# One RWKV-7 layer's key stage: a chain without GpSimd products, decays a tile ahead, and the triangles of the later heads by ranges of chunks

## The chip, the cores and the metric

The kernel runs on one core of a Trainium2 chip. The metric is the device time of one execution in microseconds (us); lower is better. The core has a matrix engine (TensorE, PE in the rows; PEld is its weight load), three elementwise engines (VectorE or DVE, ScalarE or ACT, GpSimd or POOL) and a sync engine (SyncE or SP) that does nothing but issue DMAs. Each engine has a queue of its own that it works off in order; DMAs can also be issued by ACT and POOL, and then stand in their queues.

## The reference

A decoder step of two layers over a prompt of 1024 tokens and 8 sampled tokens; the change lies in the first layer, RWKV-7 time mixing, with 32 heads of 64 channels. Cut to what matters here:

```python
r, k, v, z = einsum('pbtd,pde->pbte', mixed, w_in)          # four projections, 1024 -> 2048
w_log = -softplus(-(w0 + tanh(xw @ w1) @ w2)) - 0.5
decay = exp(-exp(w_log)); a = sigmoid(a0 + (xa @ a1) @ a2)
kk = k * k_k; kk = kk / max(norm(kk), 1e-12)                # per head
k = k * (1 + (a - 1) * k_a)
def step(S, (r, w, k, v, a, b)):                            # a = -kk, b = kk * a
    sa = S @ a
    S = S * w + outer(sa, b) + outer(v, k)
    return S, S @ r
S_fin, y = scan(step, S0, ...)                              # 1024 steps, per head
bonus = sum(rh * kh * r_k) * vh
```

The kernel does the scan in 32 chunks of 32 tokens. Inside a chunk the step is solved with the inverse of a unit triangular 32x32 matrix per head and chunk ("the triangles"), 32 x 32 of them.

## The kernel before

The layer runs in stages: r, v, then k with everything that the recurrence needs (the stage of the change), then the recurrence over 32 chunks, with the projection z spread between its steps as filling for PE. All projections are fp32 products made of three fp32r matmuls (high and low halves).

**The loop of k.** Channels are split into 16 tiles `ct` of 128 (two heads each). One pass of the loop (`for ct in range(KI - 1)`) does three tiles' work at once: `kproj(ct + 1)` (24 steps of three matmuls, spread by `steps`) and `ua(ct + 1)` (the two small projections `u` for decay and a) on PE for the next tile; the elementwise chain of tile ct; `score` (products of the rows, tile `sc`), `rows` (transposes, `tr`) and `bonus` (`bo`) of tile ct - 1. The chain of a tile: `norm` (sums of squares `ss`, maximum on VectorE, logarithm and exponential on ScalarE, each with a table load), `newkey`, `decay2` (running products of the decays over a chunk), `raw_rows`, `unit`, `unit2`, `unit_rows`; they write the rows `RA` and `BK`, which exist once. `unit` also issues the product r*k of `bonus` on GpSimd (line 821); `bonus` of the tile reads it one pass later. The program order is written by hand, and no scheduler moves anything.

**The triangles.** Tile pairs (4 heads x 32 chunks = 128 partitions) are inverted together by `inverse`: 31 steps of one multiplication (L1081) and one addition (L1083) on blocks of up to 256 elements per partition. Seven pairs run on GpSimd, a step at three of four places in `steps`, the eighth on VectorE after the loop (the tail). A pair is loaded from `n_d` and stored to `u_d` or `u2_d`.

**Into the recurrence.** `phase_r` loads, for each chunk, `xs_d` and `ra_d` (tile `xz`), `u_d`/`u2_d` (tile `U`) and `v_d` (into tile `st`). 24 of the steps of z (`ZK`) are done in the tail and 27 (`ZPRE - ZK`) ahead of the first chunk. `sample_step`, the 8 sampled tokens' state update on GpSimd and VectorE, advances by one step at each of six places of a chunk.

## Time and profile before

| | |
|---|---|
| time, median of 3 runs | 2971.76 us (2968.67 to 2973.62) |
| the profiled execution: its own time | 2943.64 us |
| its span, first to last instruction | 2941.9 us |
| busy: PE / PEld / DVE / ACT / POOL | 2696.3 / 2418.5 / 1672.7 / 1361.2 / 1430.5 us |
| the loop of k, tile 0's logarithm to tile 15's | 463.7 us |
| PE, DVE, POOL busy in it | 380.4, 402.6, 368.6 us |

The profiled execution is 28.1 us (0.9%) below the median of the timed runs. The busy time of PE is modelled from pipelined records, so it overstates how close PE is to its peak. Tiles are named by number: "tile 5" is the pass of the loop with ct = 5.

### The profile page before, as it was taken

How to read it: one execution, taken by the hardware profiler on the slowest of the kernel's cores; microseconds unless marked ns; L12 is line 12 of the kernel's file. 1: busy time of each engine (PE TensorE's matmuls, PEld its weight loads, DVE VectorE, ACT ScalarE, POOL GpSimd, SP SyncE). 2: the span in 40 equal slices, each digit the busy share in tenths (PEclk: the TensorE clock that was granted, in tenths of full speed). 3: DMA queues.
4: the chain of work that ended last, by engine and by line, in shares of the span. 5: the costliest groups of instructions: out<-in, count | busy, mean ns of one | idle time of the engine just before them, and what ended most of it. 6: DMA issues, size and time to landing. Idle time of an engine off the chain costs nothing.

```text
span 2941.9 us, 64866 instructions
## 1 busy us (share of the span) xinstructions
PE 2696.3 (92%) x26386; PEld 2418.5 (82%) x26386; DVE 1672.7 (57%) x2952; ACT 1361.2 (46%) x2886; POOL 1430.5 (49%) x1385
## 2 busy tenths in 40 slices
PE   7999998878786788888879999999999999899998
PEld 7999997766675677767769989999999999666897
DVE  7232117989797756666574144127777777533414
ACT  7232226767675444445454335225555555333423
POOL 3322121699999566663245455313444433475342
PEclk9999999989898899999989999999999999999999
DMA  4332334667677899999777552322111111586525
GB/s 157 120 126 76 96 88 113 162 145 174 155 162 190 206 223 218 227 227 210 175 228 225 173 123 78 107 83 83 54 56 54 56 52 55 157 274 201 179 90 187
DMA packets 567501, 423.80 MB, mean 144 GB/s; under 512 B 176260, under 2 KB 515649, under 8 KB 567074
## 3 DMA queue, kind: packets, MB, share of 16 engines
q1 hardware_dynamic: 473954, 336.06, 42.5%
q10 hardware_dynamic: 79648, 38.42, 4.9%
q0 software_dynamic: 13600, 45.16, 4.9%
q8 instruction: 208, 3.41, 0.5%
q14 instruction: 91, 0.75, 0.1%
HBM read 281.69 MB, written 133.35 MB: 141 GB/s over the span
## 4 chain that ended last, share of the span: by engine, by line
PE 57%; POOL 7%; DVE 7%; DMA 5%; issue 4%; ACT 3%; SPq 1%; ACTq 0%; DVEq 0%; POOLq 0%
PE p L62 8%; PE zb L62 6%; PE sc L62 6%; PE bo L62 5%; PE wop L62 4%; PE o L62 4%; POOL Xt L1081 2%; POOL X L1083 2%; PE s L62 2%; PE q L62 2%; PE pt L2156 2%; PE v L62 2%; PE k L62 1%; PE pt L2575 1%; PE bt L62 1%
## 5 line engine op out<-in xcount | busy, mean ns | idle before, releaser
L76 POOL TENSOR_TENSOR wl<-wr,wh 128x1024 fp32r<-128x1024 f32 x32 | 84.3, 2654 | 288.0 <-ACT wh L71 269.5
L1081 POOL TENSOR_TENSOR Xt<-N,X 128x31 f32<-128x31 f32 (+15 forms) x217 | 187.0, 862 | 27.2 <-DMA N<-n_d 11.0
L1083 POOL TENSOR_TENSOR X<-X,Xt 128x31 f32<-128x31 f32 (+15 forms) x217 | 183.8, 847 | 17.0
L71 ACT CAST pth<-pt 128x256 fp32r<-128x256 f32 (+1 forms) x320 | 108.2, 355 | 128.8 <-DVE ptl L76 74.8
L1289 DVE TENSOR_TENSOR st<-s,gC 64x512 f32<-64x512 f32 x128 | 88.2, 689 | 131.6 <-PE s L62 129.2
L62 PE MATMUL p<-mh,w3h 128*128 128x344 f32 x384 | 149.6, 390 | 6.2 <-issue 5.0
L76 DVE TENSOR_TENSOR ptl<-pt,pth 128x256 fp32r<-128x256 f32 (+1 forms) x320 | 120.9, 391 | 27.0 <-ACT pth L71 25.0
L62 PE MATMUL p<-ml,w3h 128*128 128x344 f32 x384 | 130.8, 341 | 5.1 <-issue 2.9
L62 PE MATMUL p<-mh,w1h 128*128 128x344 f32 x360 | 134.9, 375 | 0.0
L62 PE MATMUL p<-mh,w3l 128*128 128x344 f32 x384 | 127.1, 337 | 3.7 <-issue 3.7
L62 PE MATMUL r<-mh,wh 128*128 128x344 f32 x384 | 124.7, 325 | 4.6 <-ACT tf L483 4.6
L62 PE MATMUL r<-mh,wl 128*128 128x344 f32 x384 | 124.1, 323 | 0.0
L62 PE MATMUL r<-ml,wh 128*128 128x344 f32 x384 | 123.9, 323 | 0.0
L2139 ACT ACTIVATE pr<-sc,mx 128x128 f32<-128x128 f32 (+7 forms) x128 | 95.4, 745 | 53.1 <-DVE mx L2136 51.6
L62 PE MATMUL p<-mh,w1l 128*128 128x344 f32 x360 | 119.9, 333 | 0.0
L62 PE MATMUL p<-ml,w1h 128*128 128x344 f32 x360 | 119.8, 333 | 0.0
L2136 DVE TENSOR_REDUCE mx<-sc 128x1 f32<-128x128 f32 (+7 forms) x128 | 96.7, 755 | 3.2
L1305 ACT COPY y<-y 32x256 f32<-32x256 f32 x256 | 93.2, 364 | 10.7 <-PE y L62 7.1
L1276 ACT COPY st<-sa 32x256 f32<-32x256 f32 x128 | 46.4, 362 | 111.1 <-PE sa L62 100.7
L1950 DVE TENSOR_TENSOR zbr<-zb,RS 128x384 f32<-128x384 f32 (+1 forms) x48 | 24.6, 515 | 126.1 <-PE zb L62 123.8
L62 PEld LDWEIGHTS s<-st,xz 128*64 128x64 f32 x2048 | 72.6, 148 | 27.9 <-issue 20.9
L2041 POOL TENSOR_TENSOR qp<-qp,rope 128x256 f32<-128x256 f32 (+1 forms) x30 | 22.4, 747 | 145.8 <-DMA qsw<-qp 122.4
(1237 smaller groups left out, 9944.9 us busy)
## 6 DMA issues: line engine op xcount, KB each, us to landing
xs_d<-XS SPq DMA_DIRECT2D x64, 512.0 KB, 5.9
xz<-xs_d SPq DMA_DIRECT2D x64, 512.0 KB, 9.0
wr<-in_a_w_in_dram SPq DMA_DIRECT2D x17, 1024.0 KB, 6.1
ra_d<-RA SPq DMA_DIRECT2D x32, 512.0 KB, 7.3
...
```

Of the source, the lines that this page charges most:

```text
L62: PE.matmul(out, lhsT=lhsT, rhs=rhs, start=start, stop=stop)
L71: ACT.copy(out, in_)
L76: (eng or V).tensor_tensor(out, in_, hi_.bitcast(F32), ALU.subtract)
L1081: eng.tensor_tensor(t3, N_[:, s_:s_ + 1, s_ + 1:].to_broadcast([P, a, b]), X_[:, r0:r1, s_:s_ + 1].to_broadcast([P, a, b]), ALU.mult)
L1083: eng.tensor_tensor(X_[:, r0:r1, s_ + 1:], X_[:, r0:r1, s_ + 1:], t3, ALU.add)
L1276: (V.tensor_copy if j % 2 else ACT.copy)(d, pa[j % 2][ts(j, 32)])
L1289: V.tensor_tensor(ST[s_][1 - c % 2][rows, qs, :], p3[rows], gC[rows, qs, c:c + 1].to_broadcast([64, 8, 64]), ALU.mult)
L1305: ACT.copy(ys[B][ts(ci, 32), a:a + 2].rearrange("p a s d -> p (a s d)"), p_[ts(j, 32), 0:256])
L2136: V.tensor_reduce(mx, sc[:, :W], AX.X, ALU.max, negate=True)
L2139: ACT.activation(pr[:, :W], sc[:, :W], AF.Exp, bias=mx, accum_out=sm)
L2156: PE.transpose(pt[:, ts(q, P)], pr[:, ts(g + q, P)], ident)
L2575: PE.transpose(p_[:, ts(r, P)], pg[:, r, ts(c, P)], ident)
```

## The change

Eight things are changed. (1) The product r*k goes from GpSimd to VectorE, to the end of the pass (`rk`). (2) GpSimd cuts the low halves of k's weights (`w1l`) instead of VectorE. (3) The decays: a running sum (`CS`) on VectorE and two exponentials on ScalarE replace two exponentials and two running products; they, and the first half of `newkey`, are made for tile ct + 1 at the end of pass ct. (4) The small projections' low weights are laid out over 128 rows instead of 64. (5) `rows` leaves PSUM by one copy per group instead of four, into a tile `TR` of its own, and `xs_d` becomes two arrays with 64 elements for each channel row and chunk. (6) `score` and `rows` stand group by group in the pass. (7) The triangles of tiles 0 to 7 are made in the loop, four tiles at a time (`GROUPS`), with two triangles behind each other in every instruction; those of tiles 8 to 15 are sorted by ranges of 8 chunks, two ranges on VectorE in the tail and two on GpSimd beside the recurrence (`side`), ahead of `sample_step`. (8) The chunk's load reads `xs_d` by four DMAs instead of two.

```diff
-    xs_d = scr("xs_d", (2, NC, 64, P * KI))
+    xs_d = [scr(f"xs{i}_d", (2, KI, 64, NC, 64)) for i in range(2)]
...
-    u_d = scr("u_d", (NC, 4, C, 6, C))
-    u2_d = scr("u2_d", (NC, 2, 4, C, C))
+    u_d = scr("u_d", (NC, 4, C, 4, C))
+    u2_d = [scr(f"u2_{i}_d", (8, 4, C, 4, C)) for i in range(4)]
...
-                lo(b_, raw[:, 4 * hf:4 * hf + 4], a)
+                lo(b_, raw[:, 4 * hf:4 * hf + 4], a, G if i == 1 else V)
...
+            def lcut2(ct):
+                lo(st[ct]["l2"], st[ct]["l2r"], st[ct]["s2"])
...
-                        mm(p_[:, :NQ], d["s2"][i], th2[i][:, nsl[n]], True, False)
-                        mm(p_[:, :NQ], d["l2"][me], th2[i][me, nsl[n]], False, True)
+                        mm(p_[:, :NQ], d["s2"][:, i], th2[i][:, nsl[n]], True, False)
+                        mm(p_[:, :NQ], d["l2"][:, i], th2[i][:, nsl[n]], False, True)
...
-                ACT.activation(Wp[:, :, 1:33], c3(TW), AF.Exp, bias=cneg, scale=-0.5 * CDEC)
-                ACT.activation(Wi[:, :, 1:33], c3(TW), AF.Exp, bias=cpos, scale=0.5 * CDEC)
+                ACT.activation(CS[:, :, 1:33], c3(TW), AF.Identity, bias=ones[:, 0:1])
...
-                V.tensor_tensor_scan(fl(Wp), fl(Wp), fl(E0), 0.0, ALU.mult, ALU.add)
-                V.tensor_tensor_scan(fl(Wi), fl(Wi), fl(E0), 0.0, ALU.mult, ALU.add)
-                V.tensor_copy(gC[:, ct, :], Wp[:, :, 32])
...
+                V.tensor_tensor_scan(fl(CS), fl(E0), fl(CS), 0.0, ALU.mult, ALU.add)
+                ACT.activation(fl(Wp), fl(CS), AF.Exp, scale=-0.5 * CDEC)
+                ACT.activation(Wi, CS[:, :, 1:33], AF.Exp, scale=0.5 * CDEC)
+                ACT.activation(gC[:, ct, :], CS[:, :, 32], AF.Exp, scale=-0.5 * CDEC)
...
+                GG = st[ct]["GG"] = kp.tile([P, T], F32, tag="GG", name=f"GG{ct}")
+                ACT.activation(GG, st[ct]["TA"], AF.Identity, bias=dv[:, 3, ct:ct + 1], scale=dv[:, 2, ct:ct + 1])
...
-                V.tensor_scalar(GG, TA, dv[:, 2, ct:ct + 1], dv[:, 3, ct:ct + 1], ALU.mult, ALU.add)
-                V.tensor_scalar(TA, TA, -0.5, -0.5, ALU.mult, ALU.add)
-                V.tensor_tensor(GG, GG, d["K"], ALU.mult)
+                V.tensor_tensor(d["GG"], d["GG"], d["K"], ALU.mult)
...
-                G.tensor_tensor(d["K"][:, :S], d["R"][:, :S], d["GG"][:, :S], ALU.mult)
+            def rk(ct):
+                d = st[ct]
+                V.tensor_tensor(d["K"][:, :S], d["R"][:, :S], d["GG"][:, :S], ALU.mult)
...
-                V.tensor_tensor(d["TA"], d["TA"], d["RN"], ALU.mult)
+                V.scalar_tensor_tensor(d["TA"], d["TA"], 1.0, d["RN"], ALU.add, ALU.mult)
...
-                        SY.dma_start(n_d[ct, s_, HC[hf]].rearrange("c s t -> s c t"), d["nts", hf][r0:r0 + 32])
+                        nt = d["nts", hf][r0:r0 + 32]
+                        if ct < 8:
+                            SY.dma_start(n_d[ct, s_, HC[hf]].rearrange("c s t -> s c t"), nt)
+                            continue
+                        for i in range(2):
+                            SY.dma_start(n2_d[2 * hf + i, ct - 8, s_].rearrange("c s t -> s c t"), nt[:, ts(i, 8)])
...
-                for u in range(2):
...
-                    ACT.copy(x4[64:128, :, u, :], v4[src, :, 0, :])
-                    ACT.copy(x4[0:64, :, u, :], v4[src, :, 1, :])
...
+                ACT.copy(d["TR", hf][:, :, ts(g % 2, 4)], p_.rearrange("p (m s d) -> p s m d", m=4, s=2))
...
-                        SY.dma_start(xs_d[s_, HC[hf]][:, :, ts(ct, P)].rearrange("c r t -> r c t"),
-                                     d["XS", hf][64 * s_:64 * s_ + 64])
+                        SY.dma_start(xs_d[1][s_, ct][:, HC[hf]], d["XS", hf][64 * s_:64 * s_ + 64])
+                        for u in range(2):
+                            SY.dma_start(xs_d[0][1 - s_, ct][:, c0 + 8 * u:c0 + 8 * u + 8], d["TR", hf][ts(u, 64), s_])
...
-                    if u % 4 != 3:
-                        next(pend[0], None)
+                    due[0] += rate[0]
+                    while due[0] >= 1:
+                        due[0] -= 1
+                        istep()
...
+            GROUPS = {4: [(0, 0), (0, 1)], 8: [(0, 2), (0, 3)]}
+
+            def whole(qs, eng=G):
+                for _ in range(3):
...
+                while late:
+                    late.pop(0)()
+                rate[0] = 0.36
...
+                yield from inverse(qs, (*bufs, ivp.tile([P, C * C // 2], F32, tag="Xt", name=f"Xt{q}")), eng, late)
...
+                nm = norm(ct)
                 if p >= 0:
                     score(p, 0)
+                    rows(p, 0)
+                    bonus(p)
+                steps(kpr, 2)
+                run(take(nm, 2))
+                steps(kpr, 1)
+                run(nm)
+                newkey2(ct)
...
                     score(p, 1)
...
+                    rows(p, 1)
+                steps(kpr, 2)
...
                 raw_rows(ct, 0)
...
                 unit(ct)
...
-                if ct % 2 == 0 and p >= 0:
-                    run(pend[0])
-                    fresh = whole(p // 2)
-                    next(fresh)
...
                 unit2(ct)
                 unit_rows(ct, 0)
                 ra_store(ct, 0)
+                steps(kpr, 2)
+                if p >= 0:
+                    score(p, 2)
+                    rows(p, 2)
+                steps(kpr, 3)
+                if p >= 0:
+                    score(p, 3)
+                    rows(p, 3)
+                if ct in GROUPS:
+                    iq.append(whole(GROUPS[ct]))
+                if late and not iq:
+                    late.pop(0)()
...
                 raw_rows(ct, 1)
                 unit_rows(ct, 1)
                 ra_store(ct, 1)
+                rk(ct)
                 sample(ct)
                 rload(ct + 1)
+                for u in range(6):
+                    steps(kpr, 1)
+                    next(up)
+                run(up)
+                if ct + 2 < KI:
+                    lcut(ct + 2)
+                decay(ct + 1)
+                steps(kpr, 2)
+                newkey(ct + 1)
+                if ct + 2 < KI:
+                    lcut2(ct + 2)
+                decay2(ct + 1)
...
+                steps(kpr, 6)
...
+            iv7 = whole([(1, 0), (1, 1)], V)
+            for _ in range(4):
+                next(iv7)
...
             run(iv7)
-            late[1]()
...
+            late.pop(0)()
...
+    def inverse(qs, bufs, eng, late):
...
+        n = len(qs)
+        N_, X_ = (t_.rearrange("p n (a b) -> p n a b", b=C) for t_ in bufs[:2])
+        xf, tm = bufs[1:]
+        for i, (by_chunk, q) in enumerate(qs):
+            src = n2_d[q] if by_chunk else n_d[2 * q:2 * q + 2]
+            SY.dma_start(bufs[0][:, i], src.rearrange("k s c a b -> (k s c) (a b)"))
+        eng.memset(xf, 0.0)
+        eng.memset(xf[:, :, 0:1024:33], 1.0)
         yield
...
-                    eng.tensor_tensor(t3, N_[:, s_:s_ + 1, s_ + 1:].to_broadcast([P, a, b]),
-                                      X_[:, r0:r1, s_:s_ + 1].to_broadcast([P, a, b]), ALU.mult)
-                    eng.tensor_tensor(X_[:, r0:r1, s_ + 1:], X_[:, r0:r1, s_ + 1:], t3, ALU.add)
...
+            a, b = s_ + 1, C - 1 - s_
+            t4 = tm[:, :n * a * b].rearrange("p (n a b) -> p n a b", n=n, b=b)
+            eng.tensor_tensor(t4, N_[:, :, s_:s_ + 1, s_ + 1:].to_broadcast([P, n, a, b]),
+                              X_[:, :, 0:a, s_:s_ + 1].to_broadcast([P, n, a, b]), ALU.mult)
+            eng.tensor_tensor(X_[:, :, 0:a, s_ + 1:], X_[:, :, 0:a, s_ + 1:], t4, ALU.add)
...
-            for j in range(4):
...
-                    G.dma_start(u2_d[:, q - 6, j], X_[ts(j, 32)])
+            for i, (by_chunk, q) in enumerate(qs):
+                for j in range(4):
+                    if by_chunk:
+                        for x in range(4):
+                            rows = slice(8 * (4 * x + j), 8 * (4 * x + j) + 8)
+                            {0: (SY, ACT), 1: (G, G)}.get(q, (SY, SY))[j % 2].dma_start(u2_d[q][:, j, :, x], X_[rows, i])
+                    else:
+                        SY.dma_start(u_d[:, j, :, q], X_[ts(j, 32), i])
...
-                    SY.dma_start(X[rows, :, 128 - 128 * s_:256 - 128 * s_], xs_d[s_, c].rearrange("r (a t) -> r a t", t=P))
+                    o = 128 - 128 * s_
+                    for i, x in enumerate((c // 16 * 16 + c % 2 * 8 + c % 16 // 2, c)):
+                        SY.dma_start(X[rows, :, o + 64 * i:o + 64 * i + 64], xs_d[i][s_, :, :, x].rearrange("a r t -> r a t"))
...
-                    SY.dma_start(U[:, 0:6], u_d[c].rearrange("j a q t -> (j a) q t"))
+                    SY.dma_start(U[:, 0:4], u_d[c].rearrange("j a q t -> (j a) q t"))
...
-                    SY.dma_start(Us[c][:, 6:8], u2_d[c].rearrange("q j a t -> (j a) q t"))
+                    SY.dma_start(Us[c][:, 4:8], u2_d[c // 8][c % 8].rearrange("j a q t -> (j a) q t"))
...
-            sp = rx.enter_context(tc.tile_pool(name="spl", bufs=1, side="right", reuse_waits="tile"))
-            sg = sample_step(sp, lambda n: psum("tr", n, 1), osT, SM)
...
+            def side():
+
+                with ExitStack() as vx:
+                    vp = vx.enter_context(tc.tile_pool(name="ivr", bufs=1, side="right", reuse_waits="tile"))
+                    for r in (2, 3):
...
+                        out = []
+                        yield from inverse([(1, r)], bufs, G, out)
+                        yield
+                        yield
+                        out[0]()
+                sp = rx.enter_context(tc.tile_pool(name="spl", bufs=1, side="right", reuse_waits="tile"))
+                yield from sample_step(sp, lambda n: psum("tr", n, 1), osT, SM)
...
-                    next(sg, None)
+                    run(take(sg, 2 if c > 11 and i % 2 else 1))
```

On GpSimd, in the loop of k, before (a pair's triangles, and the product of tile 9; `N`, `X`, `Xt` are a triangle, its inverse and a scratch tile):

```order
L1081 TENSOR_TENSOR Xt3_7014<-N3_7012,X3_7013 128x255
L1083 TENSOR_TENSOR X3_7013<-X3_7013,Xt3_7014 128x17x15
L821 TENSOR_TENSOR K9_6804<-R9_7047,GG9_7193 128x1024
L1081 TENSOR_TENSOR Xt3_7014<-N3_7012,X3_7013 128x252
L1083 TENSOR_TENSOR X3_7013<-X3_7013,Xt3_7014 128x18x14
```

and now, around tile 11's weights:

```order
L1107 TENSOR_TENSOR Xt0203_6907<-N0203_6905,X0203_6906 128x270
L1109 TENSOR_TENSOR X0203_6906<-X0203_6906,Xt0203_6907 128x2x5x27
L76 TENSOR_TENSOR w1l11_0_7156<-w1r11_6961,w1h11_0_7136 128x512
L1107 TENSOR_TENSOR Xt0203_6907<-N0203_6905,X0203_6906 128x312
L1109 TENSOR_TENSOR X0203_6906<-X0203_6906,Xt0203_6907 128x2x6x26
L1107 TENSOR_TENSOR Xt0203_6907<-N0203_6905,X0203_6906 128x350
```

The product is gone from the queue, the low weights stand in it, and the blocks are two triangles wide (128x270 is 2 x 135).

On VectorE, the end of a pass, before (tile 3; `XS` is the next pass):

```order
L838 COPY SM_117<-GG3_5169 128x8
L76 TENSOR_TENSOR w1l5_1_5408<-w1r5_5182,w1h5_1_5406 128x512
L73 CAST l2h0_5_5440<-l2r5_5112 64x128
L76 TENSOR_TENSOR l2l5_5442<-l2r5_5112,l2h0_5_5440 64x128
L73 CAST l2h1_5_5441<-l2r5_5112 64x128
L76 TENSOR_TENSOR l2l5_5442<-l2r5_5112,l2h1_5_5441 64x128
L855 TENSOR_TENSOR XS3_0_5457<-sc3_0_5459,ctab_75 128x8x64
```

and now:

```order
L825 TENSOR_TENSOR K3_4778<-R3_4977,GG3_5041 128x1024
L842 COPY SM_122<-R3_4977 128x8
L842 COPY SM_122<-RN3_5120 128x8
L842 COPY SM_122<-GG3_5041 128x8
L843 TENSOR_SCALAR SM_122<-TA3_4985 128x8
L76 TENSOR_TENSOR l2l5_5324<-l2r5_5074,l2h5_5323 128x256
L798 SCALAR_TENSOR_TENSOR CS_4228<-E0_4229,CS_4228 128x1056
L860 TENSOR_TENSOR XS3_0_5373<-sc3_0_5375,ctab_80 128x512
```

The weights' cuts have left, the product r*k has come, and the running sum of tile 4 stands ahead of the next pass; `CS` waits for ScalarE, which reads the small projections.

On ScalarE, after the loop, where the eighth triangle's step ends, before:

```order
L872 COPY XS15_1_9451<-tr15_3_9573 64x4x64
L873 COPY XS15_1_9451<-tr15_3_9573 64x4x64
L1041 COPY bT_9654<-bo_4260 32x256 x4
L767 COPY zrow0_9680<-p3_0_0_9384 128x344
L767 COPY zrow0_9680<-p3_0_1_9388 128x344
L767 COPY zrow0_9680<-p3_0_2_9392 128x344
```

and now (`u2_0` takes the inverses of chunks 0 to 7, `X1011`):

```order
L880 COPY TR15_1_9132<-tr15_2_9127 128x2x256
L880 COPY TR15_1_9132<-tr15_3_9134 128x2x256
L1118 DMA u2_0_d_70<-X1011_9056 8x32x32 x8
L1068 COPY bT_9244<-bo_4264 32x256 x4
L769 COPY zrow0_9270<-p3_0_0_8941 128x344
L769 COPY zrow0_9270<-p3_0_1_8945 128x344
L769 COPY zrow0_9270<-p3_0_2_8949 128x344
```

Eight stores that wait for the last triangle now stand ahead of the copies of `bo` on ScalarE; eight more stand on SyncE and sixteen on GpSimd.

## Rows read from the trace of the kernel before

**Rows 1.** Busy time by stretch: tile 1, tile 5, the loop, the recurrence

```profile
core 0: us, PE busy (x) PEld busy (x) DVE busy (x) ACT busy (x) POOL busy (x), PEclk, DMA share, GB/s
490.70:515.80 25.10, 24.57 (x244) 20.08 (x242) 23.52 (x37) 21.39 (x44) 2.75 (x1) 1.00 0.73 169
601.70:630.80 29.10, 26.18 (x242) 21.53 (x242) 27.12 (x36) 21.63 (x43) 27.00 (x30) 0.94 0.75 166
467.40:931.10 463.70, 380.44 (x3536) 309.00 (x3535) 402.63 (x523) 315.33 (x625) 368.59 (x403) 0.91 0.65 156
...
1060.00:1480.00 420.00, 369.09 (x8153) 306.21 (x8151) 270.86 (x464) 204.09 (x520) 219.48 (x146) 0.94 0.91 210
```

**Rows 2.** Waits of PE in the loop: total, times, longest

```profile
PE bo L62 <- POOL K L821: 53.3, 9, 13.7
PE ss L62 <- DVE RN L783: 23.0, 10, 5.0
```

**Rows 3.** Timeline of VectorE and GpSimd in tile 1: start, duration

```profile
502.82 2.75 POOL L821 TENSOR_TENSOR K<-R,GG 128x1024 f32<-128x1024 f32 x1 [20.57 <-DVE RN L819]
...
503.26 3.41 DVE L825 TENSOR_TENSOR TA<-TA,RN 128x1032 f32<-128x1032 f32 x1
```

**Rows 4.** Timeline of PE in tile 13, around a pair of small products

```profile
876.20 0.32 PE L62 MATMUL u<-th,l2h 128*128 128x344 f32 x1
876.45 0.42 PE L62 MATMUL u<-th,l2l 64*128 64x344 f32 x1
876.80 0.42 PE L62 MATMUL p<-mh,w1h 128*128 128x344 f32 x1
```

**Rows 5.** Groups of ScalarE in tile 1: busy us, mean ns

```profile
L873 ACT COPY XS<-tr 64x256 f32<-64x256 f32 x8 | 2.9, 368 | 0.1
...
L71 ACT CAST w1h<-w1r 128x512 fp32r<-128x512 f32 x2 | 1.2, 618 | 0.0
L790 ACT ACTIVATE Wp<-TW,cneg 128x1024 f32<-128x1024 f32 x1 | 1.1, 1149 | 0.0
...
L785 ACT ACTIVATE RN<-RN 128x1032 f32<-128x1032 f32 x1 | 1.1, 1071 | 0.0
```

**Rows 6.** Groups of VectorE in tile 1

```profile
L798 DVE TENSOR_TENSOR_SCAN Wi<-Wi,E 128x1056 f32<-128x1056 f32 x1 | 2.3, 2332 | 0.0
...
L819 DVE SCALAR_TENSOR_TENSOR RN<-K,vecA,RN 128x1032 f32<-128x1032 f32 x1 | 1.3, 1284 | 0.0
```

**Rows 7.** The triangles on GpSimd, from the page's groups

```profile
L1081 POOL TENSOR_TENSOR Xt<-N,X 128x31 f32<-128x31 f32 (+15 forms) x217 | 187.0, 862 | 27.2 <-DMA N<-n_d 11.0
L1083 POOL TENSOR_TENSOR X<-X,Xt 128x31 f32<-128x31 f32 (+15 forms) x217 | 183.8, 847 | 17.0
```

**Rows 8.** The product r*k in the loop, a group of GpSimd

```profile
L821 POOL TENSOR_TENSOR K<-R,GG 128x1024 f32<-128x1024 f32 x15 | 37.3, 2484 | 67.5 <-DVE RN L819 67.5
```

**Rows 9.** Timeline of VectorE in the tail

```profile
971.73 0.67 DVE L1081 TENSOR_TENSOR Xt<-N,X 128x31 f32<-128x31 f32 x1
...
991.42 0.42 DVE L1081 TENSOR_TENSOR Xt<-N,X 128x256 f32<-128x256 f32 x1
```

**Rows 10.** Timeline of PE and GpSimd in the tail

```profile
972.44 1.16 PE L1045 MATMUL boT<-ctab,bT 32*128 32x32 f32 x8
...
986.79 0.32 PE L62 MATMUL p<-mh,w3h 128*128 128x344 f32 x1
...
1003.84 1.94 POOL L1091 DMA_DIRECT2D u_d<-X  x4 [8.62 <-DVE X L1083]
```

**Rows 11.** State products on VectorE: 1000 to 1050, then all (first to last start)

```profile
L1289 DVE TENSOR_TENSOR st<-s,gC x10: 682/689/695, 1007.6 to 1047.8; 64x512 f32<-64x512 f32 x10
...
L1289 DVE TENSOR_TENSOR st<-s,gC x128: 682/690/696, 1007.6 to 1486.8; 64x512 f32<-64x512 f32 x128
```

**Rows 12.** DMA queues, 1200 to 1300: packets, MB, time as share of 16 engines

```profile
q1 hardware_dynamic: 26511, 17.29, 75.7%
q10 hardware_dynamic: 13947, 4.88, 21.1%
```

156 lines of the change are left out of this document (57 added, 99 removed).

## The prediction

> **What bounds the kernel now.** I read the busy times by stretch first, then the waits of PE in the loop of k, then the timeline around the waits, since the change lies in that loop, the tail behind it and the recurrence. The loop takes 463.7 us for 15 periods, 30.9 each, with PE busy for 380.4 and GpSimd for 368.6 [rows 1]. In tile 1, where GpSimd has only the product r*k, a period lasts 25.1 and PE is busy for 24.6; in tile 5, where it also makes triangles, 29.1, with GpSimd busy for 27.0 [rows 1]. So there are two limits: PE where GpSimd is quiet, and GpSimd where it is not. The waits name the link: PE stood for 53.3 us in nine waits at `bonus` until the product on GpSimd was done, and for 23.0 in ten at the sums of squares until VectorE had read the ones before [rows 2]. The product is short (2.48 on the mean [rows 8]) but stands behind the steps of a triangle, and everything behind `bonus` in PE's queue stands behind it.
>
> GpSimd also slows VectorE. In tile 1 the product ran from 502.82 to 505.57, and a multiplication that VectorE began at 503.26 ended at 506.67, 1.1 after the product [rows 3]; its like takes 1.28 [rows 6], so it stood for some 2.1. The Trainium skill ("SBUF — State Buffer", section "SBUF: two separate sides") says that GpSimd and VectorE instructions with two inputs in SBUF take turns at a shared port for whole instructions; these two rows agree.
>
> **The change part by part.**
>
> *The product on VectorE.* It costs VectorE about 1.28 (same width as in [rows 6]) and takes away the 2.1 of standing. The 53.3 of waiting at `bonus` go, unless VectorE is late in turn: the product now ends pass ct, and `bonus` reads it at the start of pass ct + 1, behind `score` and `rows`.
>
> *PE per tile.* A small product starts its high half at 876.20, its low half at 876.45 and hands over at 876.80: 0.60 for two matmuls, and the one behind lasts 0.42 [rows 4]. In the tail 81 matmuls of the same width take 986.79 - 973.6 (972.44 + 1.16), 0.16 each [rows 10]. If the 64-row weights make the difference, 128 rows save 0.60 - 0.32 on the pair and 0.1 behind it, 0.38 times 6 = 2.3 per tile; the bounds are nothing and 2.3, and I take all, since the gap stands only at that shape. Four blocks of `score` and `rows` instead of two cost two more changes of shape each way, 0.5 by the same rows. PE would need 24.6 - 2.3 + 0.5 = 22.8.
>
> *ScalarE per tile.* It is busy for 21.4 [rows 1]. Sixteen copies at 0.37 (5.9), two exponentials of 1.15 and two small casts (0.6) go; four copies of 512 columns come (0.62 each at most, as the cast of that width), a copy into `CS` and two exponentials (1.15 each), `newkey` (1.07), a small exponential and a cast (0.7) [rows 5]. 21.4 - 8.8 + 7.7 = 20.3.
>
> *The ring from tile to tile.* ScalarE's queue is now closed through VectorE in two places. After the exponential of `norm`, VectorE makes `unit` and `unit2` (1.28 each), two rows and the next mask (0.65 each, half the width), 4.5 in all [rows 6], before ScalarE can copy `score`'s third group; it has 1 us of copies meanwhile, so it stands for 3.5. The running sum takes 2.33 [rows 6] between `CS` and the exponentials of the decays, with 1.3 of other ScalarE work beside it, so it stands for 1. The square of the next K is queued behind that. A period is then 20.3 + 4.5 = 24.8, say 24.9, above PE's 22.8. VectorE's own sum falls below it: 23.5 [rows 1] less one running product (2.33), the standing (2.1), the weights' cuts and the two scalings that ScalarE or a fused instruction takes over (some 3), plus the product: 17 to 18. So I expect PE to wait for ScalarE's and VectorE's chain for 2 us in a quiet tile; the bounds of a quiet period are 22.8 (all of that hidden) and 26.
>
> *Triangles in the loop.* They now fill tiles 4 to 11. Now 62 instructions take 0.855 each on the mean of 176 elements [rows 7]; the product is the row for 1024, 2.48 [rows 8]. On the line between, 352 elements cost 1.19, so four tiles' triangles cost 74 against 106 for two pairs. At 0.36 steps of 24 per tile they spread over four tiles: 18.4 each, plus two cuts of 512 at 1.35, 21.1. That fits a period. In the middle, where a block has 512 elements, 8.6 steps cost 24 and the cuts 2.7: just over it, so the weights may come late by a few us once per group. VectorE pays for GpSimd's company: 27.1 against 23.5 [rows 1], a sixth, on the 7 us of it that lie in the ring. 24.9 + 1.2, and 1 for late weights: 27.0 with the bounds 25 and 30. GpSimd no longer delays `bonus`; what is queued behind a late weights' cut is PE's next tile, and that is the last link between them.
>
> The loop: 7 x 24.9 + 8 x 27.0 = 390, **-73** (with the bounds' ends -104 to -42).
>
> *Ahead of the loop* the running sum and the exponentials of tile 0 stand uncovered in part: **+2**.
>
> *Tail, VectorE.* Two running products (4.7) and two scalings leave the stretch ahead of the last triangle, the product comes: -5. The triangle itself took from 971.73 to 1003.5 [rows 9, 10]. 256 elements cost 0.42 late in it [rows 9]; most of that scales with the elements, so twice the blocks at, by estimate, 0.55 for each of 62 with their gaps are 34: +2. Together **-3** (-10 to +4).
>
> *Tail, behind the triangle.* Before, its stores waited on GpSimd (8.62 us [rows 10]) and nothing was queued behind them but a fill. Now eight wait on ScalarE and eight on SyncE. Behind them on ScalarE stand the copies of `bo`, the evacuation of z and the fills for the first chunk; behind `bo`'s transposes on PE stand 27 steps of z, which before ran from 973.6 to 986.79 beside the triangle [rows 10]. On SyncE the loads of chunks 0 and 1 stand behind them. So what took 4.0 us (1003.5 to the first state product at 1007.6 [rows 10, 11]) now takes 5 for the stores' issues (by estimate: four took 1.94 [rows 10], and the second four wait for the first to land), 1.5 for the copies, 1.2 for the transposes, 13.2 for the 27 steps and 4.0 as before, 25 in all: **+21** (+5, should PE have other work, to +28).
>
> *First chunks.* Two chunks took 40.2, against 479.2 / 31.5 = 15.2 for one on the mean [rows 11]; the loads now have those 20 us of PE's work as cover: **-8** (0 to -10).
>
> *Recurrence.* Two triangles of 62 instructions (53 us each at 0.855) on GpSimd, whose busy share is half [rows 1]; the step of the samples follows in the later chunks. The state products on VectorE took 682 to 696 ns whatever stood on GpSimd [rows 11], so I cost it at nothing (0 to +10). The loads: the same bytes in pieces of 256 B instead of 512 B. Queue 10, which carries `ra_d` in 256 B pieces, moved 4.88 MB in 21.1% of 16 x 100 us, 14.5 bytes per ns; queue 1, with the 512 B pieces, 17.29 MB in 75.7%, 14.3 [rows 12]. Time goes by bytes, so: nothing. The Trainium skill ("DMA: Bandwidth & Descriptors", section "Specifications") wants at least 512 B per transfer for line rate; these two rows do not show that loss, and by the rule alone the sum would end on the other side, as in the third rival.
>
> Sum: -73 + 2 - 3 + 21 - 8 = -61. Against the profiled execution's 2943.6 us that is 2883; it lies 28.1 below the median of the runs, and I carry the difference over: 2971.8 - 61 = **2911 us**.
>
> **The rivals.**
>
> *The ring is shorter than I add up* (copies overlap, ScalarE is never behind): quiet periods at PE's 22.8, busy ones at 25: 7 x 22.8 + 8 x 25 = 360, -104 in the loop, -92 in all: 2880. For it: ScalarE has 20.3 of work in such a period. Against it: its queue is in order and has two waits for VectorE.
>
> *GpSimd stays the bound of busy tiles*: double blocks cost double (1.71), 106 per group and 11 of cuts with waits, 117 in four tiles, 29.3, as tile 5 is now. 8 x 29.3 + 7 x 24.9 = 409, -55, and -43 in all: 2929. For it: the mean of 0.855 holds the turns with VectorE, and those grow with an instruction's length. Against it: VectorE has a quarter less to do.
>
> *Slower: the small pieces cost as much as large ones.* At 14.3 bytes per ns and engine a chunk's 1 MB takes 4.6 us of 16 engines; in half pieces at the price of whole ones 9.2. The engines are busy for 91% of the recurrence [rows 1], 13.8 of 15.2 us, so a chunk would need 18.4: +3.2 times 32 = +102, and +41 in all: 3013. It decides against the change from a price of 1.6 times per byte. Against it: [rows 12], where 256 B pieces go at the rate of 512 B ones.
>
> *No change*: the tail's exposed steps and some recurrence waits eat the loop's gain; that needs the upper bound of each, -42 + 28 + 10.
>
> **Chances.** The sum as worked out, 2895 to 2920: 0.5. Shorter ring: 0.2. GpSimd still the bound: 0.2. Slower pieces or a tail and a recurrence at their worst: 0.07, no change: 0.03. The range that leaves out no more than 2 in 10 is 2868 to 2943. A difference under 0.2% (6 us) cannot be told from none. Faster 0.91, same 0.03, slower 0.06.
>
> **What would show it.** Right: no wait of PE for a product on GpSimd; small products at 0.16 a matmul; a period near 25 in tiles 1 to 3 and 12 to 14 and near 27 in between, with ScalarE busy for some 20; a first state product some 25 us behind the tail's last triangle, and PE idle beside that triangle; chunks of 15 us. Wrong: waits for `w1l` of many us in tiles 5 to 11; periods of tiles 1 to 3 that are not shorter than 25.1, or at 23; queue shares of the DMAs that grow with the same bytes; chunks that lengthen while GpSimd makes triangles.

## The result and the profile after

The changed kernel takes 3009.5 us (median of 4 runs, 3005.8 to 3013.7) against 2972.7 us for the kernel before: a ratio of 1.0118 (95% interval 1.0088 to 1.0149). It is 36.8 us slower; the forecast was 61 us faster.

By the marks of the front part (the logarithm of tile 0 and of tile 15, the first state product of chunk 0 and of chunk 31), from the two profiled executions:

| stretch, us | before | after | difference | forecast |
|---|---|---|---|---|
| ahead of the loop | 467.4 | 472.1 | +4.7 | +2 |
| loop of k, 15 periods | 463.7 | 400.7 | -63.0 | -73 |
| tail, to the first state product | 76.5 | 105.9 | +29.4 | +18 (-3 and +21) |
| chunks 0 to 15 | 250.1 | 278.3 | +28.2 | -8 |
| chunks 16 to 31 | 223.2 | 262.0 | +38.8 | 0 |
| to the start of chunk 31's product, in sum | 1480.9 | 1519.1 | +38.2 | -61 |

What lies behind is the same code in both. It took 1461.0 us in the profiled execution before and 1492.7 after, and 1486 to 1499 in the fourteen kernels below. So the execution before, which lay 28 us below the median of its runs, was probably short there and not in the stretches of the table; no second trace of that kernel is kept, so this is not shown. The 38.2 agree with the 36.8 of the medians.

Busy time by stretch in the changed kernel: tiles 2 and 6, the loop, the tail, chunks 0 to 15 and 16 to 31 (start and end, length, then busy us of each engine with its instructions, granted clock, DMA share, GB/s):

```profile
516.80:540.30 23.50, 22.73 (x244) 20.07 (x246) 17.76 (x25) 18.66 (x33) 3.56 (x2) 1.00 0.72 200
619.20:650.10 30.90, 26.16 (x252) 23.18 (x248) 28.24 (x26) 19.11 (x35) 29.65 (x19) 0.89 0.54 150
472.10:872.80 400.70, 355.48 (x3521) 311.33 (x3520) 319.65 (x377) 281.05 (x489) 214.34 (x160) 0.94 0.67 180
872.80:978.70 105.90, 48.37 (x549) 43.06 (x548) 59.00 (x99) 31.36 (x51) 13.46 (x20) 0.74 0.63 155
978.70:1257.10 278.40, 215.44 (x4663) 178.45 (x4664) 136.83 (x234) 117.72 (x299) 151.37 (x178) 0.90 0.83 188
1257.10:1519.10 262.00, 210.25 (x4365) 173.49 (x4365) 165.89 (x262) 109.74 (x282) 157.80 (x111) 0.89 0.79 189
```

Against [rows 1]: in the quiet tile VectorE and ScalarE have 18 to 19 us of work, and PE is busy for 22.73 of 23.5. ScalarE's two stands for VectorE, in its timeline of that tile, are there:

```profile
525.94 0.37 ACT L861 COPY nts<-sc 128x256 f32<-128x256 f32 x1 [3.69 <-DVE XS L860]
...
536.06 1.08 ACT L799 ACTIVATE Wp<-CS 128x1056 f32<-128x1056 f32 x1 [1.11 <-DVE CS L798]
```

18.66 of work, 3.69 and 1.11 make 23.5: ScalarE's ring sets the period, and PE stands 0.8 below it. In the busy tile GpSimd is the fullest engine (29.65 of 30.9), with VectorE close behind it (28.24, for work that takes 17.76 in the quiet tile).

In the recurrence the DMA engines, 91% busy before, are now idle for about a fifth of the time: it is not their rate that holds it.

The waits of PE in the loop, which answer to [rows 2], show none at `bonus`:

```profile
PE u L62 <- ACT nts L861: 21.0, 12, 4.2
PE ss L62 <- ACT nts L861: 8.9, 4, 4.2
PE p L62 <- POOL w1l L76: 5.0, 2, 4.5
```

GpSimd's groups of triangle steps in the loop (busy us, mean ns of one, idle before them), which answer to [rows 7]:

```profile
L1107 POOL TENSOR_TENSOR Xt<-N,X 128x62 f32<-128x62 f32 (+15 forms) x62 | 80.1, 1291 | 14.6 <-DMA N<-n_d 9.8 <-issue 1.1
L1109 POOL TENSOR_TENSOR X<-X,Xt 128x62 f32<-128x62 f32 (+15 forms) x62 | 74.9, 1208 | 4.9
L76 POOL TENSOR_TENSOR w1l<-w1r,w1h 128x512 fp32r<-128x512 f32 x28 | 48.0, 1713 | 144.0 <-ACT w1h L71 106.9 <-DMA xs_d<-TR 24.7 <-DMA xs_d<-XS 12.4
```

The tail, from the timelines of VectorE, ScalarE, SyncE and PE (start, duration, idle time before and what ended it):

```profile
908.18 0.22 DVE L1107 TENSOR_TENSOR Xt<-N,X 128x62 f32<-128x62 f32 x1 [5.68 <-DMA N<-n_d]
...
942.65 0.27 DVE L1109 TENSOR_TENSOR X<-X,Xt 128x62 f32<-128x62 f32 x1
...
942.94 12.09 ACTq L1118 DMA_DIRECT2D u_d<-X  x8
955.07 1.53 ACT L1068 COPY bT<-bo 32x256 f32<-32x256 f32 x4 [52.41 <-DMA u_d<-X]
...
942.94 11.98 SPq L1118 DMA_DIRECT2D u_d<-X  x8
954.97 3.45 SPq L1268 DMA_DIRECT2D xz<-xs_d  x2
...
955.49 1.58 PE L1072 MATMUL boT<-ctab,bT 32*128 32x32 f32 x8 [50.70 <-ACT bT L1068]
```

The triangle takes the 34 us that were forecast. ScalarE and SyncE then need 12 us to issue the stores, and PE, idle for 50.7 us, begins the 27 steps of z only behind them.

Most of the loss was forecast nowhere. Two chunks of the first half take 29.2 and 29.8 us. The first, in the timelines of SyncE, GpSimd and VectorE:

```profile
1058.27 0.43 SPq L1278 DMA_DIRECT2D U<-u_d  x1
1060.65 14.40 SPq L1118 DMA_DIRECT2D u_d<-Xr  x16
1075.09 0.37 SPq L1100 DMA_DIRECT2D Nr<-n_d  x1
...
1077.47 0.95 POOL L1101 MEMSET Xr<- 128x1024 f32 x1 [22.65 <-DMA u_d<-Xr]
...
1080.60 2.34 POOL L1381 TENSOR_TENSOR y<-y,lnw 128x1024 f32<-128x1024 f32 x1
1082.90 1.90 POOL L1382 TENSOR_TENSOR vb<-vb,bon 128x1024 f32<-128x1024 f32 x1
...
1084.83 0.76 DVE L1388 TENSOR_TENSOR y<-y,vb 128x512 f32<-128x512 f32 x1 [16.75 <-POOL vb L1382]
...
1086.42 1.41 DVE L1320 TENSOR_TENSOR st<-s,gC 64x512 f32<-64x512 f32 x2
```

and in the waits of PE in the same stretch:

```profile
PE ot L1396 <- DVE y L1388: 13.3, 1, 13.3
```

This is a chain through four queues in order. The first triangle on GpSimd is ready, but its sixteen stores stand on SyncE behind loads and need 14.4 us (6.3 of issuing; the rest passes between them, where an issue waits for the semaphore of an earlier transfer); the second triangle's `memset` wants the same tile and waits 22.65 us for them; the products of the group norm stand behind the `memset` on GpSimd; VectorE's sum waits for these products, and behind it stand the state products of the next chunk. The second chunk, on ScalarE and SyncE:

```profile
1161.49 0.45 ACT L774 COPY zrow<-p 128x344 f32<-128x344 f32 x1 [0.21 <-PE p L62]
1177.69 0.33 ACTq L775 DMA_DIRECT2D zT_d<-zrow  x1
1178.07 0.73 ACT L1307 COPY st<-sa 32x256 f32<-32x256 f32 x2 [16.13 <-DMA u_d<-Xr]
...
1170.65 9.25 SPq L1118 DMA_DIRECT2D u_d<-Xr  x16
```

ScalarE stands at the store of a z tile, which has nothing to do with the triangle. In the trace the transfers of SyncE and ScalarE take the same eight semaphores in turn (those of GpSimd take eight others), and the one that this store waits for is that of a triangle store which SyncE issues only at 1175.26.

### The profile page after: what moved, and what is told of

The parts are those of the page before. It is cut to its first block, busy times and chain, and to the rows that moved or that the text cites. A ratio compares the mean times of both kernels' runs of the same rounds, so it can differ in the third digit from the quotient of the medians.

```text
span 3011.8 us, 64861 instructions
## 1 busy us (share of the span) xinstructions
PE 2688.8 (89%) x26386; PEld 2430.7 (81%) x26386; DVE 1591.0 (53%) x2794; ACT 1319.3 (44%) x2726; POOL 1300.2 (43%) x1216
## 4 chain that ended last, share of the span: by engine, by line
PE 48%; DMA 7%; DVE 7%; ACT 3%; POOL 3%; issue 3%; SPq 1%; another core or an unknown queue 1%; ACTq 1%; DVEq 0%; POOLq 0%
PE zb L62 6%; PE sc L62 5%; PE bo L62 5%; PE wop L62 4%; PE o L62 4%; PE p L62 3%; PE q L62 2%; PE pt L2202 2%; PE pt L2621 2%; PE v L62 2%; PE s L62 1%; PE ssc L62 1%; DMA xz<-ra_d 1%; PE k L62 1%; PE bt L62 1%
## 5 line engine op out<-in xcount | busy, mean ns | idle before, releaser
L76 POOL TENSOR_TENSOR w1l<-w1r,w1h 128x512 fp32r<-128x512 f32 x30 | 50.5, 1683 | 152.3 <-ACT w1h L71 115.2
L2554 POOL DMA_INDIRECT pg<-in_cache_ckv_dram,idx x64 | 60.8, 950 | 97.2 <-issue 43.6
L62 PEld LDWEIGHTS s<-st,xz 128*64 128x64 f32 x2048 | 75.1, 150 | 29.8 <-DVE st L1307 11.8
L62 PE MATMUL s<-st,xz 128*64 128x64 f32 x2048 | 86.8, 239 | 12.6 <-DVE st L1307 9.3
## 6 DMA issues: line engine op xcount, KB each, us to landing
rT_d<-rr ACTq DMA_DIRECT2D x16, 516.0 KB
R<-rT_d SPq DMA_DIRECT2D x16, 516.0 KB
```

Of the source, the lines that this page charges most:

```text
L62: PE.matmul(out, lhsT=lhsT, rhs=rhs, start=start, stop=stop)
L76: (eng or V).tensor_tensor(out, in_, hi_.bitcast(F32), ALU.subtract)
L2554: G.indirect_dma_start(t_.rearrange("p r c -> p (r c)"), None, A[nm].rearrange("n (q r) c -> (n q) (r c)", r=4), off)
```

## The experiments

All kernels are the changed kernel with the edit shown, or an earlier experiment's with one more. The times of the stretches are from one profiled execution each, by the marks above; ratios are to the kernel before on the same chip, with 95% intervals.

| kernel | loop | tail | chunks 0-15 | 16-31 | median us | ratio |
|---|---|---|---|---|---|---|
| before | 463.7 | 76.5 | 250.1 | 223.2 | 2972.7 | 1 |
| changed | 400.7 | 105.9 | 278.3 | 262.0 | 3009.5 | 1.0118 (1.0088-1.0149) |
| 1: one store | 398.9 | 91.8 | 245.3 | 256.3 | 2963.7 | 0.9979 (0.9965-0.9993) |
| 2: other pace | 398.5 | 103.5 | 280.2 | 252.5 | 3003.3 | 1.0113 (1.0092-1.0134) |
| 3: 1 and 2 | 400.6 | 92.2 | 263.6 | 252.4 | 2975.7 | 1.0025 (1.0010-1.0041) |
| 4: r*k on GpSimd | 418.7 | 104.9 | 279.0 | 260.3 | 3022.6 | 1.0172 (1.0152-1.0191) |
| 5: 1, two loads of 512 B | 408.1 | 94.8 | 239.9 | 235.0 | 2953.2 | 0.9928 (0.9902-0.9955) |
| 6: 1, four loads of 512 B | 408.7 | 93.7 | 243.7 | 229.3 | 2939.9 | 0.9873 (0.9844-0.9903) |
| 7: 1, first loads on ScalarE | 398.8 | 93.4 | 242.2 | 258.1 | 2962.4 | 0.9970 (0.9952-0.9988) |
| 8: 5 and 7 | 408.2 | 95.9 | 238.5 | 235.3 | 2942.6 | 0.9877 (0.9844-0.9910) |
| 9: 1, xs half on ScalarE | 398.8 | 91.6 | 281.9 | 264.6 | 3004.2 | 1.0115 (1.0077-1.0154) |
| 10: 512 B, sixteen stores | 409.7 | 105.3 | 257.2 | 225.1 | 2967.6 | 0.9998 (0.9981-1.0015) |
| 11: 64-row products | 431.8 | 105.3 | 279.0 | 255.5 | 3038.7 | 1.0217 (1.0175-1.0260) |
| 12: 6, other tail order | 409.2 | 94.0 | 240.8 | 229.1 | 2932.2 | 0.9864 (0.9824-0.9905) |
| 13: 6 in 256 B pieces | 407.4 | 92.3 | 255.1 | 260.3 | 2973.3 | 1.0022 (1.0003-1.0041) |
| 14: 6, first loads on GpSimd | 407.3 | 82.8 | 236.7 | 228.2 | 2923.7 | 0.9857 (0.9824-0.9891) |

**1. One store for each triangle.** The order of partitions is changed so that the load of a chunk still finds heads and rows in one step:

```diff
-    n2_d = scr("n2_d", (4, 8, 2, 8, C, C))
+    n2_d = scr("n2_d", (4, 4, 8, 2, 2, C, C))
...
-                        for x in range(4):
-                            rows = slice(8 * (4 * x + j), 8 * (4 * x + j) + 8)
-                            {0: (SY, ACT), 1: (G, G)}.get(q, (SY, SY))[j % 2].dma_start(u2_d[q][:, j, :, x], X_[rows, i])
+                    SY.dma_start(u2_d[q].rearrange("x c j a t -> (x c j) (a t)"), bufs[1][:, i])
```

> The changed kernel, with each triangle by chunks stored in one transfer instead of sixteen (N and X hold the sixteen chunk-and-head pairs in another order of partitions, so that 128 partitions go out at once; the same for the two of the tail, two stores instead of 32). Theory A (the stores: sixteen issues stand in SyncE's queue ahead of the loads, they take all eight DMA semaphores twice, ScalarE's store of z and GpSimd's next memset wait for them): the two chunks of 29.2 and 29.8 us fall to 15 to 18, the stretch from first to last state product from 540 to 510-515, the tail from 105.9 to 93-97 (its stores took 12.1), the time to 2965-2975. Theory B (the sample step, squeezed into the last twenty chunks at two steps a time): only the tail's 10 go, chunks 5 and 11 stay near 29. Theory C (the half-size pieces of the loads slow every chunk): the same as B for the chunks.

The two long chunks are gone (17.0 and 21.2, the second above the 15 to 18 expected), chunks 0 to 15 fall by 33 us to 245.3, the tail by 14, the time by 46. Theory A holds for these stretches. It stops there: chunks 16 to 31 keep 256.3 of their 262.

**2 and 3. The pace of the side work**, alone and with one store.

```diff
-                    run(take(sg, 2 if c > 11 and i % 2 else 1))
+                    run(take(sg, 2 if c < 5 or (c > 22 and i % 3 == 2) else 1))
```

> The changed kernel, with the side work at two steps a slot in chunks 0 to 4, then one, and two in each third slot from chunk 23 on, instead of one until chunk 11 and two in each second slot from there. Theory B: chunks 16 to 31, 262 us against 223 before, come back to 225-235, since GpSimd and VectorE no longer get a second step of the samples beside the group norm; the time falls by 25-40 to 2970-2985. Theory A alone: chunks 16 to 31 stay within 10 us of 262, and the two stalls behind the stores only move to earlier chunks (at 3 and 6). Theory C: nothing moves.

> Both edits in one kernel. If A and B each hold a part: the recurrence from first to last state product at 475-490, as the 473 of before, the tail at 93-97, and with the loop's 400 the time at 2925-2940, below the kernel before. If the small pieces were the cause, the recurrence stays above 520.

Chunks 16 to 31 gain 9.5 and 3.9 us instead of 27 or more, and the first half loses what it had (263.6 against 245.3 in the third, whose recurrence of 516.0 us is far from the 475 to 490 expected). In the second the long chunks only move, to chunks 3 and 6 (27.0 and 25.1). Theory B falls; the pace as it was is the better one.

**5 and 6. The loads in 512 B pieces**, as two transfers and as four.

```diff
-    xs_d = [scr(f"xs{i}_d", (2, KI, 64, NC, 64)) for i in range(2)]
+    xs_d = scr("xs_d", (2, KI, 64, NC, 2, 64))
...
 # 5
+                    SY.dma_start(X[rows, :, o:o + 128], xs_d[s_, :, :, c].rearrange("a r i t -> r a (i t)"))
 # 6
+                    for i in range(2):
+                        SY.dma_start(X[rows, 8 * i:8 * i + 8, o:o + 128], xs_d[s_, 8 * i:8 * i + 8, :, c].rearrange("a r i t -> r a (i t)"))
```

> The kernel with one store for each triangle (the first experiment), and the two halves of a chunk's xs block side by side in DRAM, so that a chunk's loads are two transfers of 512 B pieces on SyncE again instead of four of 256 B pieces. Theory D (SyncE's queue is the limit of the chunks with the sample step: each issue waits for one of eight DMA semaphores, which ScalarE's transfers share, and two more issues a chunk make it late): chunks 16 to 31, 256 us there, fall to 225-235, the first sixteen stay at 240-246, the time falls by 20-30 to about 2938. Theory E (the sample step itself, on GpSimd and VectorE at two steps a slot, is the limit): chunks 16 to 31 stay at 250-258 and the time at 2960. The loop's stores are now in 256 B pieces, as the profile's rows have it at the same rate per byte: no more than 3 us there.

> The same layout, with the load cut into four transfers again (eight head pairs each, 512 B pieces). It differs from the fifth run by the number of issues alone, from the first by the size of pieces alone. Theory D: as the first run, chunks 16 to 31 at 250-258. Theory C (small pieces): as the fifth run.

Both bring chunks 16 to 31 down by more than 20 us, and four transfers do it as well as two. So it is not the number of issues (theory D) but the pieces or their place in DRAM. The loop pays 10 us for it, three times what I allowed. Its stores into the common tensor, now in 256 B pieces, are what changed there; in all seven kernels with this layout the loop takes 407 to 410.

**13. The same place in DRAM, small pieces.**

```diff
-                        SY.dma_start(X[rows, 8 * i:8 * i + 8, o:o + 128], xs_d[s_, 8 * i:8 * i + 8, :, c].rearrange("a r i t -> r a (i t)"))
+                        SY.dma_start(X[rows, :, o + 64 * i:o + 64 * i + 64], xs_d[s_, :, :, c, i].rearrange("a r t -> r a t"))
```

> The sixth run's kernel, with the same place of the xs blocks in DRAM, the same stores and the same four loads a chunk, but each load taking 64 columns of all sixteen head pairs (256 B pieces, 1024 of them) instead of 128 columns of eight (512 B pieces, 512 of them). If the size of pieces is the cause: chunks 16 to 31 go from 229 back to 250-260 and the time to 2960-2968. If the two separate tensors of the changed kernel (their place in DRAM) were the cause, chunks 16 to 31 stay at 228-236 and the time at 2940.

Place, stores and count of loads are the sixth run's, and chunks 16 to 31 go back from 229.3 to 260.3, the time up by 33. A load here also brings half of the columns for all head pairs instead of all columns for half of them; but in the fifth kernel too each load is for all of them, and chunks 16 to 31 take 235.0 there, so this is worth no more than 6 of the 31 us. The size of the pieces is the cause in these chunks. The busy times of chunks 16 to 31 in the sixth kernel:

```profile
1216.80:1446.20 229.40, 200.11 (x4365) 164.83 (x4365) 165.57 (x262) 110.23 (x283) 158.46 (x111) 0.95 0.91 212
```

and in the thirteenth:

```profile
1226.20:1486.50 260.30, 209.26 (x4366) 172.37 (x4365) 166.23 (x261) 109.37 (x280) 157.39 (x111) 0.90 0.78 189
```

The queue that carries these loads, in the same stretch (packets, MB, share of 16 engines), in the sixth:

```profile
q1 hardware_dynamic: 61181, 37.10, 68.8%
```

and in the thirteenth:

```profile
q1 hardware_dynamic: 91296, 38.24, 60.8%
```

The issues of the loads on SyncE (ns, min/median/max; first and last start), in the sixth:

```profile
L1266 SPq DMA_DIRECT2D xz<-xs_d x55: 573/633/1724, 1218.0 to 1422.2; - x55
```

and in the thirteenth:

```profile
L1266 SPq DMA_DIRECT2D xz<-xs_d x56: 574/792/4178, 1230.6 to 1468.1; - x56
```

A byte takes the engines no longer: 37.10 MB in 0.688 x 16 x 229 us are 14.7 bytes per ns, 38.24 in 0.608 x 16 x 260 are 15.1. What differs is that the engines stand idle for 22% of the time instead of 9%, and that a load holds SyncE longer (up to 4.2 us). SyncE's waits in these stretches tell the same: in the sixth kernel most is 39.7 us for PE to be done with a buffer, and 16.8 for transfers of `ra_d` that ScalarE issued; in the thirteenth these are 11.0 and 56.6, with 25.3 for ScalarE's stores of z. Its queue, early with large pieces, is late with small ones. Which of this is cause and which effect, the two traces don't say.

**9. Half of the small loads issued by ScalarE**, to see whether SyncE's time is what they cost.

```diff
-                        SY.dma_start(X[rows, :, o + 64 * i:o + 64 * i + 64], xs_d[i][s_, :, :, x].rearrange("a r t -> r a t"))
+                        (ACT if i and c > 2 else SY).dma_start(X[rows, :, o + 64 * i:o + 64 * i + 64], xs_d[i][s_, :, :, x].rearrange("a r t -> r a t"))
```

> The first experiment's kernel (one store; four loads a chunk in 256 B pieces), with two of the four xs loads issued by ScalarE from chunk 3 on. The pieces are the same. Theory D' (small pieces cost by the time that their issue holds SyncE: the third and fourth in a row took 1.67 and 1.22 us against 0.64 with 512 B pieces, and what stands behind them, the v for the group norm and the samples' state, comes late): with SyncE relieved, chunks 16 to 31 come down from 256 to 230-240. Theory C' (the transfer of small pieces itself is slow, whoever issues them): 250-260.

Worse in both halves of the recurrence, the first by ScalarE's own queue: in chunks 0 to 15 PE waits for `rhs`, a copy that stands behind the issues.

```profile
PE sa L62 <- ACT rhs L1294: 44.0, 14, 10.2
```

This tells nothing on D' against C'; by which of them small pieces cost stays open.

**10. 512 B pieces with the sixteen stores.** The edit of the sixth run alone.

> The changed kernel with the loads in 512 B pieces (as in the sixth run) but with its sixteen stores for each triangle. If the two causes add up: the stalls behind the stores stay (two chunks of 27 to 30 us, tail near 106), chunks 16 to 31 fall from 262 to 230-238, the recurrence is 505-515 and the time 2975-2990. If the small pieces were also what made the stores late, the stalls shrink below 20.

The long chunks stay (27.7 and 27.3), the tail too, and chunks 16 to 31 fall to 225.1. The two causes are separate, but they do not add up (the recurrence is 482.3, below the 505 to 515 expected): of the 540.3 us from first to last state product, large pieces alone take 58.0, one store alone 38.7, both 67.3, to 473.0. Before it was 473.3.

**7, 8, 12 and 14. The tail's order.** The loads of chunks 0 and 1 (7, 8) or of chunk 0 (12, where the tail's two triangles also go out in one store) on ScalarE; in 14 those of chunk 0 on GpSimd:

```diff
-                    SY.dma_start(ST[0][c % 2][96:128], v_d[0, ts(c, 32)])
+                    (SY if c else G).dma_start(ST[0][c % 2][96:128], v_d[0, ts(c, 32)])
...
 (and so for st of the other half, xs and ra of chunk 0)
```

> The first experiment's kernel, with the loads of chunks 0 and 1 (xs, r/a and v of chunk 0) issued by ScalarE, which is idle beside the tail's triangle, instead of SyncE, where they stand behind the triangle's store. If that order is what is left of the tail (90.5 us, of which the 34.3 in which PE waits for v_d), the tail falls to 74-79 and the time by 12-16, to about 2950. If the loads cannot start earlier (their buffers still in use), nothing moves.

> One store, two loads a chunk and the first loads on ScalarE in one kernel. If D holds and the tail's order too: tail 74-79, recurrence 470-480, time 2915-2930, faster than the kernel before by 1.3 to 1.8%. If E holds: 2945-2955.

> The sixth run's kernel (one store for each triangle, 512 B pieces), with the tail's two triangles in a single store and the loads of chunk 0 alone on ScalarE, so that none of these takes the DMA semaphore on which SyncE's store of the triangle waits (in the eighth run the loads of v on ScalarE stood 15 us for just that semaphore, and 27 steps of z behind them). If that semaphore is what kept the tail at 92 to 95: the 27 steps run beside the triangle, the tail is 76-80, the time 2924-2930. If the tail stays at 90 or more, something else holds it.

> The sixth run's kernel, with chunk 0's loads (xs, r/a, v) issued by GpSimd, which is idle in the tail and whose transfers use semaphores of their own. If the semaphores that SyncE's and ScalarE's transfers share are what holds the tail (in the twelfth run the second load of v stood on ScalarE until a load of SyncE behind the triangle's store had landed): the 27 steps of z run beside the triangle, the tail falls from 92 to 76-82, the time to 2922-2930. If it stays at 90 or more, the order of loads is not what holds the first chunk.

On ScalarE nothing is gained. In the seventh and eighth runs the loads that are ready stop at a semaphore; the instructions of the eighth, SyncE's stores and ScalarE's loads of v, in the order of each engine's queue (`DMAHW6` and `DMAHW7` are two of the eight semaphores):

```
544 L1115 DMA u2_0_d_69<-X1011_9055 128x1024 [waits DMAHW6_49,DVE_49]
545 L1115 DMA u2_1_d_70<-X1011_9055 128x1024 [waits DMAHW7_49]
805 L1280 DMA st0_0_9278<-v_d_62 32x1024 [waits DMAHW6_49,Activation_49]
806 L1281 DMA st1_0_9280<-v_d_62 32x1024 [waits DMAHW7_49,Activation_49]
```

and its timeline of ScalarE:

```profile
934.39 1.99 ACT L1495 COPY st<-zero 128x1024 f32<-128x1024 f32 x2
953.70 0.39 ACTq L1280 DMA_DIRECT2D st<-v_d  x1
```

ScalarE stands from 936.4 to 953.7 for two semaphores that belong to stores which wait for VectorE's triangle. With one semaphore fewer taken (12) the second load of v still stands, from 940.4 to 961.67, until a load of SyncE behind the store has landed:

```profile
940.07 0.34 ACTq L1283 DMA_DIRECT2D st<-v_d  x1
961.67 0.34 ACTq L1284 DMA_DIRECT2D st<-v_d  x1
962.05 0.45 ACT L769 COPY zrow<-p 128x344 f32<-128x344 f32 x1 [21.07 <-DMA xz<-xs_d]
```

Only on GpSimd, whose transfers have semaphores of their own, do the loads start early (14): the 27 steps of z run beside the triangle, and PE's last wait is for U, which does need it. The tail falls by 10.9 us, to 82.8 (76 to 82 expected):

```profile
PE sa L62 <- DMA U<-u_d: 18.1, 2, 17.1
```

That kernel has the lowest time of all, 2923.7 us, 1.4% below the kernel before; its interval overlaps with those of 6, 8 and 12, so only the gain over the kernel before is certain.

**4 and 11. Two terms of the loop undone**: r*k on GpSimd, and the low product on 64 rows.

```diff
 # 4
-                V.tensor_tensor(d["K"][:, :S], d["R"][:, :S], d["GG"][:, :S], ALU.mult)
+                G.tensor_tensor(d["K"][:, :S], d["R"][:, :S], d["GG"][:, :S], ALU.mult)
...
 # 11
-                        mm(p_[:, :NQ], d["l2"][:, i], th2[i][:, nsl[n]], False, True)
+                        me = slice(64 * i, 64 * i + 64)
+                        mm(p_[:, :NQ], d["l2"][me, i], th2[i][me, nsl[n]], False, True)
```

> The changed kernel, with the product r*k back on GpSimd (its place in the order kept). By the prediction's link (PE waits at the bonus for a product that stands behind triangle steps on GpSimd) the tiles with triangles (5 to 7, 10 and 11, now 30.4 to 32.3) grow to 34-37 and PE's waits at the bonus come back, 20-30 us in all; quiet tiles stay at 23.5 within 0.5. If the link was worth little in the new order (the product now has the whole of a pass), the loop stays at 400 within 5.

> The changed kernel with the second of the two small products again on 64 rows, as before. By the prediction's term of PE (0.38 us for each of six pairs) a quiet tile's PE needs 2.3 us more, and as PE then stands above the ring, periods grow from 23.5 to 25.0-25.8, the loop from 400 to 415-425, the time by 15 to 25. If the gaps around the 64-row weights hid behind other waits, the loop stays within 5 us.

With the product on GpSimd the loop grows by 18 us, but not as expected: no wait at `bonus` comes back, and it is the quiet tiles that go from 23.5 to 26.9. Timelines of GpSimd and VectorE in such a tile:

```profile
552.84 3.41 POOL L825 TENSOR_TENSOR K<-R,GG 128x1024 f32<-128x1024 f32 x1 [6.30 <-DVE RN L821]
...
553.95 2.85 DVE L833 TENSOR_TENSOR RA<-RN,Wp 128x512 f32<-128x512 f32 x1
```

A product of VectorE that takes 0.69 elsewhere takes 2.85 here, ending 0.55 behind GpSimd's. ScalarE's stand for VectorE, 3.69 in the changed kernel, is longer by as much:

```profile
558.03 0.37 ACT L861 COPY nts<-sc 128x256 f32<-128x256 f32 x1 [5.85 <-DVE XS L860]
```

and PE waits for that copy for 2.7 us in such a tile instead of 0.6. With 64 rows a quiet tile takes 25.2 instead of 23.5, all of it PE's (busy times of 25.2 us, from tile 1 into tile 2):

```profile
499.00:524.20 25.20, 25.13 (x251) 20.24 (x247) 17.87 (x26) 19.07 (x34) 3.54 (x2) 1.00 0.64 169
```

PE is busy for 2.4 more than in tile 2 of the changed kernel, and 0.8 of that fills what it had under the ring. The loop takes 31 us more, beyond the 15 to 25 expected: tiles 2 to 4 pay 1.6 each, the others from nothing to 4.7 (tile 12, with a granted clock of 0.83 instead of 0.95). That term is real.

## Why the prediction was wrong

**The step that failed is the recurrence**, costed at nothing (0 to +10) and measured at +67 to the last chunk. It failed twice. "Two triangles of 62 instructions" counted GpSimd's arithmetic and left out the 32 stores that the step issues; for the tail I had costed such stores' issues, here not. And what waits behind them was not looked for: the tile of the second triangle, the group norm behind its `memset`, the semaphore of ScalarE's store. One store for each triangle takes 38.7 us out of the recurrence (experiment 1). The last sign of being wrong that the prediction names, chunks that lengthen while GpSimd makes triangles, came: chunks 5 and 11.

**"Time goes by bytes, so: nothing"** is the other half. The rate per byte was read rightly and is the same after, yet loads in small pieces cost 28 us beside one store and 42 against the same layout (experiment 13). The third rival had the right sign and the wrong mechanism, a price per piece that would have kept the engines busy; they went idle. Its 3013 us lie next to the 3009.5 by luck (its limit of 1.6 times per byte should be 1.7; nothing hangs on it). I gave it 0.07, together with a tail and a recurrence at their worst. The Trainium skill ("DMA: Bandwidth & Descriptors", section "Specifications") asks for at least 512 B for line rate; the time goes the way of that rule here, but the rate, 15.1 against 14.7 bytes per ns, shows no loss. Setting the rule aside because one row doesn't show its loss was the mistake.

**Loop**: the mechanism held (no wait for the product, a ring, GpSimd in busy tiles) and the sum was 10 us off. Quiet tiles took 23.5 instead of 24.9: ScalarE's two stands came as forecast (3.7 and 1.1 for 3.5 and 1), its work is 18.7 instead of 20.3. Tiles 4 to 11 took 28.8 on the mean instead of 27.0. The end of the second rival came, GpSimd as the bound of busy tiles, but not its price of 1.71 for an instruction on double blocks: that took 1.25 (forecast 1.19), a cut 1.71 (1.35), and four tiles' triangles filled three tiles and were the bound there. The middle was under-costed by the sum's own line, which makes the 8.6 steps of 512 elements 26 us and not 24. And VectorE beside double blocks pays 10.5 us in tile 6, where a sixth of the 7 us in the ring was allowed. That the waits at `bonus` went away is due to the new order, not to the engine (experiment 4); what the move saves is VectorE's standing, which [rows 3] show.

**PE per tile** was right: 22.7 busy in tile 2 against 22.8 in the sum, and in experiment 11 it is busy for 2.4 more, the term of 2.3.

**Tail**: the triangle came out at -2.3 us against 72.4 before (forecast -3). Behind it the 25 us were 35.8: the stores' issues took 12.1 instead of 5, the term that was mis-sized most. The 27 steps took 15.3 instead of 13.2: after 50.7 us without work PE began them with matmuls 0.29 us apart, later 0.16; the granted clock was 0.50 from 942.9 to 955.5, the lower of its two levels. What follows them took 6.5 instead of 4.0. **Ahead of the loop**: +4.7 instead of +2. **First chunks**: -4.4 instead of -8 (the 40.2 read from [rows 11] hold one product more than two chunks, which took 39.5), since the loads stood behind the stores as well (with one store, these two chunks take 30.8, -8.7).
